# Value product copies, a weight rest and a rotary sum placed elsewhere in a two-layer encoder trunk

## The chip, the cores and the metric

The kernel runs on one core of a Trainium2 chip. The metric is the device time of one execution in microseconds (us), as the median of several runs. The engines are named as in the profile: PE is TensorE's matmuls and PEld its weight loads, DVE is VectorE, ACT is ScalarE, POOL is GpSimd and SP is SyncE, which here issues most of the transfers. PSUM is the memory that matmuls write to, and SBUF holds everything else on the core.

## The reference

Two layers over 512 tokens of width 1024, in fp32. Layer 0 mixes the tokens by neighbourhood attention with 16 heads of width 64, layer 1 by latent attention (MLA) with 16 heads, whose queries and shared key have a rotary part of width 32. In both, the mixer's output is multiplied by a gate `silu(z)` and projected. After each mixer comes a second gate that adds a projection of the per-layer input `p`.

```python
def apply_rope(x, cos, sin):
    x1, x2 = jnp.split(x, 2, axis=-1)
    ...
    return jnp.concatenate([x1 * c - x2 * s, x1 * s + x2 * c], axis=-1)

def mixer_na(xn, w_in, rpb, w_out):
    q, k, v, z = jnp.split(xn @ w_in, 4, axis=-1)
    o = neighbourhood_attention(q.reshape(shp), k.reshape(shp), v.reshape(shp), rpb)
    return (o.reshape(B, S, hd) * jax.nn.silu(z)) @ w_out

def reference(x, p, ...):
    for i in range(DEPTH):
        xn = rmsnorm(x, norm_g[i])
        y = mixer_na(...) if i % 2 == 0 else mixer_mla(...)
        h = x + y
        gate = jax.nn.sigmoid(rmsnorm(h, ple_norm[i]) @ ple_w_gate[i])
        x = h + gate * (p[i] @ ple_w_proj[i])
    return rmsnorm(x, final_norm)
```

## The kernel before, in words

**Splits.** Every fp32 product is made of three matmuls in a faster type. A matrix is split into a rounded copy (`hi`) and what is left (`lo`), and hi·hi, lo·hi and hi·lo are summed in a PSUM bank. ACT usually makes the copy. What is left, called the rest here, is one subtraction on DVE or POOL. For weights `load_w` does this: a transfer on SP's queue into a raw tile (`wraw`, three buffers), a copy on ACT (L100), a rest on POOL or, where `rest` says so, on DVE (L101).

**PSUM.** `psum(tag)` hands out the banks: two for `mm`, two for `S`, three for `T`, one for `O`. A new tile in a tag waits until the tile that had its bank has been read.

**Who sets the order.** The program is written as a Python function whose statements are in a chosen order. A scheduler with a time model then sets the order of each engine's queue from the dependencies, the priorities that follow from the order of the statements, and explicit `issue_after` ties. Within a queue an engine goes strictly in order, so an instruction that waits holds everything behind it.

**Layer 0's values.** The value projection is computed as seven products of half the size (`values_seven`, L261 to L410), after the scheme of Strassen: weights and inputs are first mixed (sums and differences), the products are numbered 1 to 7, and the four quarters of the result are put together from them by adding and subtracting whole PSUM banks. `made(p, c, ...)` splits piece c (0 or 1) of product p's weight into copy (ACT) and rest (DVE, two instructions). `product(p)` issues 24 matmuls, the first 12 into the bank of half 0 and the others into that of half 1 (L301). Products 5 and 3 add onto the banks of product 6, product 4 onto those of product 7. So before product 5 may add onto a bank of product 6, that bank's content has to be kept: `after6` copies it to SBUF on ACT (`s6`) and subtracts it from product 7's bank on DVE. `after7` adds `s1` to product 7's bank on DVE and copies the sum out on ACT (`s17`). Nearly all of these copies and rests stand on L51, the line of a helper; they are told apart by their tiles. `pair.rests(1)` makes the rests of a pair of heads' queries and keys.

**Layer 0's heads.** Sixteen heads in pairs (`na_head`, L536 to L609); heads are numbered from 0 here. A head works in two halves. PE makes scores into an `S` bank (L558, L559), DVE adds the bias and finds the maxima (L565, L568), ACT exponentiates and sums (L576), DVE takes the reciprocal of two sums at a time (L578), POOL multiplies by it (L582, two instructions for each half). PE then transposes the result into `T` banks (L594, L596), ACT and DVE split them (`ph`, `pl`, L110 and L112), and PE multiplies by the values into the `O` bank (L608). From there ACT copies (L220), DVE adds (L221), and POOL multiplies by the gate and splits (L225, L229, `oh` and `ol`). PE's queue is filled between these steps with matmuls of other work. `out_proj` (L622 to L637) loads four weight pieces for each of two column halves n, pieces c = 1 and 3 with their rests on DVE, and makes eight products (`ps_mm`, `ps_S`, `ps_T`, `ps_O`) out of `oh` and `ol`.

**Layer 1's rotary part.** For each of four groups of heads, `rope(g)` (L980 to L999) turns a PSUM tile of queries: a copy (L992, ACT), an exchange of neighbours (L993, DVE), two multiplications by the tables of cosines and sines (L994 on DVE; L995 on DVE for g = 0, else POOL), their sum (L996, POOL), the split into a copy (L997, ACT) and a rest (L998, POOL). SP then moves the parts of `rh` and `rl` to the tiles of the single heads (`qe`, `qo`, L117). The scores of the first heads of layer 1 (PE, L123, `ps_S<-ke,qe`) use them.

Of the kernel before, what the change touches and what calls it, by code (L numbers as in the profile page):

```python
# [16 lines left out]
ALU = mybir.AluOpType  # L17
# [39 lines left out]
class Trunk:  # L57
# [28 lines left out]
        return t  # L86


    def load_w(self, ap, n, extra=False, parts=1, rest=None, late=None):

        nc = self.nc
        pool = self.wx if extra else self.wp
        raw = self.wp.tile([P, 1024], F32, name="wraw", tag="wraw", bufs=3)
        tags = ("w4", "w4") if extra and self.wxn > 5 else ("whi", "wlo")
        hi, lo = (pool.tile([P, n if extra else 1024], F32R, name="whi"[:1] + t, tag=t, bufs=self.wxn if extra else 3)
                  for t in tags)
        w = n // parts
        for c in [slice(i * w, (i + 1) * w) for i in range(parts)]:
            self.last_load = nc.sync.dma_start(raw[:, c], ap[:, c])
            nc.scalar.activation(hi[:, c], raw[:, c], AF.Copy)  # L100
            f = lambda e, c=c: e.tensor_tensor(out=lo[:, c], in0=raw[:, c], in1=hi[:, c].bitcast(F32), op=ALU.subtract)  # L101
            if late is not None and c.stop == n:
                late.append(lambda: f(nc.gpsimd))
            else:
                f(rest or nc.gpsimd)
        return hi, lo


# [158 lines left out]
    def values_seven(self, pool, xT, xk, Q, pair, more):  # L267

        nc = self.nc
# [49 lines left out]
        def after7(i):  # L319
            self.dve.tensor_tensor(out=C[7, i], in0=C[7, i], in1=s1[i], op=ALU.add)  # L320
            s17[i] = copy("s17", i, C[7, i])

        def after6(i):
            s6[i] = copy("s6", i, C[6, i])
            sub(C[7, i], C[7, i], s6[i])

        def after5(i):
# [53 lines left out]
        product(7)  # L381
        pair.keys(1)
        made(5, 1, T[5][:, 1, :])
        after7(0)
        after7(1)
        made(4, 0, T[7][:, 0, :], True)
        pair.rests(1)
        product(6)
        after6(0)
        after6(1)  # L390
        made(4, 1, T[7][:, 1, :], True)
        made(3, 0, self.raw_piece(1, 2))
        product(5)
# [142 lines left out]
    def na_head(self, pool, h, sq, s0, dk, kl, vh):  # L536
# [9 lines left out]
        for half in range(2):  # L546
            sp = self.psum("S")
            for i in range(2):
                qt = 2 * half + i
                o = sp[:, i * 256:(i + 1) * 256]  # L550
                if qt == 0:
                    o = o.rearrange("p (a b) -> p a b", a=2)
                    lq = s0
                    K = lambda t: win(t, 0, P, 0, [[384, 2], [1, P]])
                else:
                    lq = sq[:, qt * P - 64:qt * P + 64]
                    K = lambda t: t[:, (qt - 1) * P:(qt + 1) * P]
                nc.tensor.matmul(o, lq, K(dk), start=True, stop=False)  # L558
                nc.tensor.matmul(o, lq, K(kl), start=False, stop=True)  # L559
            for i in range(2):  # L560
                qt = 2 * half + i
                c = slice(qt, qt + 1)
                if qt == 0:
                    for r, sc in ((slice(0, 64), slice(0, 128)), (slice(64, 128), slice(128, 256))):
                        nc.vector.tensor_tensor_reduce(out=ex[r, 0:P], in0=sp[r, sc], in1=bias[r, 0:P], scale=-1.0,  # L565
                                                       scalar=-NEG, op0=ALU.add, op1=ALU.min, accum_out=mx[r, c])
                else:
                    nc.vector.tensor_tensor_reduce(out=ex[:, ecol(qt)], in0=sp[:, i * 256:(i + 1) * 256],  # L568
                                                   in1=bias[:, P:], scale=-1.0, scalar=-NEG, op0=ALU.add, op1=ALU.min,
                                                   accum_out=mx[:, c])  # L570
            hs = slice(2 * half, 2 * half + 2)
            for i in range(2):
                qt = 2 * half + i
                e = ex[:, ecol(qt)]
                with self.tc.issue_after(self.hold):
                    self.last_exp = nc.scalar.activation(e, e, AF.Exp, scale=-1.0, bias=mx[:, qt:qt + 1],  # L576
                                                         accum_out=sm[:, qt:qt + 1])
            nc.vector.reciprocal(rc[:, hs], sm[:, hs])  # L578
            for i in range(2):
                qt = 2 * half + i  # L580
                e = ex[:, ecol(qt)]
                self.last_norm = nc.gpsimd.tensor_tensor(out=e, in0=e, in1=rc[:, qt:qt + 1].to_broadcast([P, e.shape[1]]),  # L582
                                                         op=ALU.mult)
# [21 lines left out]
        n = 0  # L605
# [16 lines left out]
    def out_proj(self, wap, oT, res, after, last_mm):  # L622
        nc = self.nc
        for n in range(2):
            ws = [self.load_w(wap[n, c], 1024, extra=n == 1 or c == 3, rest=nc.vector if self.wxn > 5 and c % 2 else None)
                  for c in range(4)]
            for u, t in enumerate(range(NT)):
                ps = self.psum(("mm", "mm", "S", "S", "T", "O", "mm", "mm")[n * NT + u])
# [313 lines left out]
    def mla_heads(self, pool, xT, cT, sets, oT):  # L942
# [42 lines left out]
        def rope(g, a0, a1):  # L985
# [7 lines left out]
            nc.vector.stream_shuffle(sw, xr, swap)  # L993
            nc.vector.tensor_tensor(out=xr, in0=psr, in1=rc_t, op=ALU.mult)  # L994
            (nc.gpsimd if g else nc.vector).tensor_tensor(out=sw, in0=sw, in1=rs_t, op=ALU.mult)  # L995
            nc.gpsimd.tensor_tensor(out=sw, in0=xr, in1=sw, op=ALU.add)  # L996
            nc.scalar.activation(rh, sw, AF.Copy)  # L997
            A["rl", g] = nc.gpsimd.tensor_tensor(out=rl, in0=sw, in1=rh.bitcast(F32), op=ALU.subtract)  # L998
            R[g] = rh, rl  # L999
# [475 lines left out]
```

## Time and profile before

| | us |
|---|---|
| median of 3 runs | 653.1 (652.88 to 653.74) |
| profiled execution | 653.56 |
| its span (first to last instruction) | 651.5 |
| PE busy | 640.2 |
| DVE busy | 427.7 |
| ACT busy | 453.4 |
| POOL busy | 408.4 |

The granted TensorE clock was 0.995 of full speed. The view of waits gives, for each group of instructions, the time that its engine sat idle, who released it, how often, and the longest. A row of the timeline has the start in us from the span's start, the time from start to end of the group, the engine, the line and the operation with its output and inputs, how many instructions are joined in the row, and in brackets the idle time before it with its releaser. Matmuls overlap, so that their starts are closer together than their durations. SPq is SP's queue of transfers: a row there is the issue.

### The profile page before, as it was taken

To read this page: it belongs to the slowest core of one execution; us is meant where nothing else is said; L and a number is where in the kernel's file an instruction comes from. 1 tells how busy PE (TensorE), PEld (TensorE's weight loads), DVE (VectorE), ACT (ScalarE), POOL (GpSimd) and SP (SyncE) were. 2 spreads that over 40 slices of the span, in tenths; PEclk is the share of its full clock that TensorE was granted. 3 is DMA by queue.
4 is the path that set the end of the run, shared out by engine and by line. 5 is a ranking of instruction groups with operands and counts; after the bars stand their busy time and mean duration, and the time that the engine had idled before them with its cause. 6 is when DMAs were issued, how large, how long until landed. Compare 5 with 4: busy or idle time off the path is not lost.

```text
span 651.5 us, 9980 instructions
## 1 busy us (share of the span) xinstructions
PE 640.2 (98%) x3299; PEld 541.9 (83%) x3299; DVE 427.7 (66%) x886; ACT 453.4 (70%) x903; POOL 408.4 (63%) x371
## 2 busy tenths in 40 slices
PE   9999999999999999999999999999999999999994
PEld 6888878888888888888999887888888888888884
DVE  6197987565665616569715514898988885474665
ACT  7575766887886733788644535897989897547855
POOL 0471006877978853797655516786969887437974
PEclk9999999999999999999999999999999999999997
DMA  9939725778958989446643245120112223683524
GB/s 326 355 124 306 217 66 179 263 205 217 229 209 217 239 178 342 147 154 188 224 140 102 78 109 156 32 75 24 49 50 66 65 84 112 229 292 126 193 65 162
DMA packets 46131, 107.41 MB, mean 165 GB/s; under 512 B 4736, under 2 KB 17792, under 8 KB 46080
## 3 DMA queue, kind: packets, MB, share of 16 engines
q1 hardware_dynamic: 34608, 87.12, 39.3%
q0 software_dynamic: 11040, 18.88, 13.6%
q10 hardware_dynamic: 432, 0.79, 0.3%
q8 instruction: 26, 0.43, 0.3%
q14 instruction: 25, 0.20, 0.1%
HBM read 95.23 MB, written 25.17 MB: 185 GB/s over the span
## 4 chain that ended last, share of the span: by engine, by line
PE 83%; POOL 1%; ACT 1%; DVE 0%; DMA 0%; issue 0%; POOLq 0%
PE ps_mm L123 27%; PE ps_S L123 10%; PE ps_mm L959 7%; PE ps_T L155 6%; PE ps_T L851 5%; PE ps_O L1071 5%; PE ps_mm L851 3%; PE ps_S L851 3%; PE ps_O L608 2%; PE ps_T L123 2%; PE ps_O L123 2%; PE ps_mm L909 2%; PE ps_T L301 2%; PE ps_T L596 2%; PE ps_S L909 1%; PE ps_S L559 1%
## 5 line engine op out<-in xcount | busy, mean ns | idle before, releaser
L101 POOL TENSOR_TENSOR wwlo<-wraw,wwhi 128x1024 fp32r<-128x1024 f32 (+5 forms) x68 | 122.3, 1810 | 93.5 <-ACT wwhi L100 41.9
L796 POOL TENSOR_TENSOR wlo<-wraw,whi 128x512 fp32r<-128x512 f32 x56 | 72.7, 1331 | 22.3 <-ACT whi L794 20.2
L1056 POOL TENSOR_TENSOR ex<-ex,rc 128x512 f32<-128x512 f32 x64 | 66.2, 1043 | 26.6 <-DVE rc L1055 22.5
L100 ACT ACTIVATE wwhi<-wraw 128x1024 fp32r<-128x1024 f32 (+5 forms) x71 | 55.1, 799 | 34.3 <-PE ps_mm L123 18.9
L1054 ACT ACTIVATE ex<-ps_S,mx 128x512 f32<-128x512 f32 x64 | 44.0, 687 | 12.6 <-DVE mx L1052 10.9
L1052 DVE TENSOR_REDUCE mx<-ps_S 128x1 f32<-128x512 f32 x64 | 43.7, 683 | 8.4 <-PE ps_S L123 7.7
L582 POOL TENSOR_TENSOR ex<-ex,rc 128x128 f32<-128x128 f32 (+1 forms) x64 | 37.5, 701 | 17.7 <-DVE rc L578 17.5
L112 DVE TENSOR_TENSOR pt_lo<-ps_T,pt_hi 128x512 fp32r<-128x512 f32 x64 | 43.1, 680 | 7.1 <-ACT pt_hi L110 6.7
L110 ACT ACTIVATE pt_hi<-ps_T 128x512 fp32r<-128x512 f32 x64 | 37.7, 594 | 3.4 <-PE ps_T L155 3.0
L155 PE MATMUL ps_T<-ident,ex 128*128 128x128 f32 x256 | 38.3, 272 | 0.0
L155 PEld LDWEIGHTS ps_T<-ident,ex 128*128 128x128 f32 x256 | 31.5, 140 | 7.5
L123 PE MATMUL ps_mm<-xh,wwhi 128*128 128x512 f32 x120 | 33.7, 404 | 0.0
L221 DVE TENSOR_TENSOR u<-ps_O,u 64x512 f32<-64x512 f32 x32 | 21.9, 685 | 17.7 <-ACT u L220 17.2
L576 ACT ACTIVATE ex<-ex,mx 128x128 f32<-128x128 f32 (+1 forms) x64 | 30.2, 473 | 4.2 <-DVE mx L565 4.1
L123 PE MATMUL ps_mm<-xl,wwhi 128*128 128x512 f32 x120 | 31.9, 395 | 0.0
L794 ACT ACTIVATE whi<-wraw 128x1024 fp32r<-128x1024 f32 x28 | 29.3, 1057 | 3.2 <-DMA wraw<-sum 2.4
L123 PE MATMUL ps_mm<-xh,wwlo 128*128 128x512 f32 x120 | 31.1, 394 | 0.0
L123 PE MATMUL ps_S<-ke,qe 96*128 96x512 f32 x96 | 28.9, 407 | 0.3 <-DMA qe<-rl 0.3
L123 PE MATMUL ps_S<-ko,qo 128*128 128x512 f32 x96 | 28.9, 409 | 0.0
L959 PE MATMUL ps_mm<-cT,wwhi 128*128 128x512 f32 x94 | 27.7, 393 | 0.0
L220 ACT ACTIVATE u<-ps_O 64x512 f32<-64x512 f32 x32 | 18.9, 591 | 12.0 <-PE ps_O L608 8.8
L225 POOL TENSOR_TENSOR u<-u,z 128x512 f32<-128x512 f32 x16 | 22.6, 1412 | 7.5 <-DVE u L221 7.5
(488 smaller groups left out, 1915.1 us busy)
## 6 DMA issues: line engine op xcount, KB each, us to landing
sum<-gate POOLq DMA_DIRECT2D x12, 1024.0 KB, 8.2
wraw<-na_qk SPq DMA_DIRECT2D x16, 512.0 KB, 4.9
wraw<-sum SPq DMA_DIRECT2D x16, 512.0 KB, 3.3
pe<-pe SPq DMA_DIRECT2D x31, 256.0 KB, 5.9
wraw<-gate SPq DMA_DIRECT2D x12, 512.0 KB, 3.3
wraw<-na_v SPq DMA_DIRECT2D x10, 512.0 KB, 3.4
sum<-sum POOLq DMA_DIRECT2D x4, 1024.0 KB, 11.1
wraw<-na_o SPq DMA_DIRECT2D x8, 512.0 KB, 4.8
```

The source lines that it names most:

```text
L100: nc.scalar.activation(hi[:, c], raw[:, c], AF.Copy)
L101: f = lambda e, c=c: e.tensor_tensor(out=lo[:, c], in0=raw[:, c], in1=hi[:, c].bitcast(F32), op=ALU.subtract)
L110: self.last_copy = self.act.activation(hi, src, AF.Copy, scale=scale)
L112: self.dve.tensor_tensor(out=lo, in0=src, in1=hi.bitcast(F32), op=ALU.subtract)
L123: last = self.last_mm = nc.tensor.matmul(out, l, r, start=i == 0, stop=i == n - 1)
L155: self.last_mm = self.nc.tensor.transpose(t[:, i * P:(i + 1) * P], b, self.ident)
L796: nc.gpsimd.tensor_tensor(out=lo[:, o], in0=raw[:, o], in1=hi[:, o].bitcast(F32), op=ALU.subtract)
L851: mm = nc.tensor.matmul(ps, l, r, start=j == 0 and p in banks, stop=j == 11 and p in (2, 3, 4), skip_group_check=True)
L959: self.last_mm = nc.tensor.matmul(PS[key], *terms[i], start=i == 0, stop=i == len(terms) - 1)
L1052: nc.vector.reduce_max(mx, sp, axis=AX.X, negate=True)
L1054: nc.scalar.activation(ex, sp, AF.Exp, bias=mx, accum_out=sm)
L1056: nc.gpsimd.tensor_tensor(out=ex, in0=ex, in1=rc.to_broadcast([P, S]), op=ALU.mult)
```

## The change

It has three edits.

1. In `values_seven` product 6 is issued ahead of product 7's adds and copies, and its two copies are split off as `copy6(i)`. The first copy now comes ahead of both `after7`, the second behind them; the subtractions of `after6` follow, and piece 0 of product 4's weight comes last.
2. `load_w` gets an argument `behind`. In `out_proj` the rest of piece (n, c) = (0, 1) is tied behind `last_rc`, the last reciprocal that a head of layer 0 has issued. (In layer 1 that reciprocal is long past.)
3. In the first rope (g = 0) the sum of the two products is taken by DVE, not by POOL.

```diff
-    def load_w(self, ap, n, extra=False, parts=1, rest=None, late=None):
+    def load_w(self, ap, n, extra=False, parts=1, rest=None, late=None, behind=None):
...
-                f(rest or nc.gpsimd)
+                with self.tc.issue_after(behind) if behind is not None else nullcontext():
+                    f(rest or nc.gpsimd)
...
+        def copy6(i):
+            s6[i] = copy("s6", i, C[6, i])
+
         def after6(i):
-            s6[i] = copy("s6", i, C[6, i])
             sub(C[7, i], C[7, i], s6[i])
...
         made(5, 1, T[5][:, 1, :])
+        product(6)
+        copy6(0)
         after7(0)
         after7(1)
+        copy6(1)
+        after6(0)
+        pair.rests(1)
+        after6(1)
         made(4, 0, T[7][:, 0, :], True)
-        pair.rests(1)
-        product(6)
-        after6(0)
-        after6(1)
         made(4, 1, T[7][:, 1, :], True)
...
-            nc.vector.reciprocal(rc[:, hs], sm[:, hs])
+            self.last_rc = nc.vector.reciprocal(rc[:, hs], sm[:, hs])
...
             ws = [self.load_w(wap[n, c], 1024, extra=n == 1 or c == 3, rest=nc.vector if self.wxn > 5 and c % 2 else None,
+                              behind=self.last_rc.ins if (n, c) == (0, 1) and self.wxn > 5 else None)
                   for c in range(4)]
...
-            nc.gpsimd.tensor_tensor(out=sw, in0=xr, in1=sw, op=ALU.add)
+            (nc.gpsimd if g else nc.vector).tensor_tensor(out=sw, in0=xr, in1=sw, op=ALU.add)
```

The lines of the changed kernel stand one to six further down than those of the kernel before (L101 stays, L221 is L222, L578 is L583, L996 is L1002).

**ACT at product 6.** This is the difference of ACT's two queues at the end of the value products. `s_846` and `s_849` before, and `s_874` and `s_877` now, are the s17 copies of product 7's two halves; `s_884` and `s_887` before, and `s_871` and `s_879` now, are the s6 copies of product 6's two halves. `whi<-W_519` is the copy of a weight piece of product 4.

```order
 L51 ACTIVATE whi<-W_539 128x1024 [waits PE_49]
-L51 ACTIVATE s_846<-ps_T 128x512 [waits DVE_49]
-L51 ACTIVATE s_849<-ps_T 128x512 [waits DVE_49]
-L51 ACTIVATE whi<-W_519 128x1024
-L51 ACTIVATE s_884<-ps_T 128x512 [waits PE_49]
-L51 ACTIVATE s_887<-ps_O 128x512 [waits PE_49]
-L51 ACTIVATE whi<-W_519 128x1024
+L51 ACTIVATE s_871<-ps_T 128x512 [waits PE_49]
+L51 ACTIVATE s_874<-ps_T 128x512 [waits DVE_49]
+L51 ACTIVATE s_877<-ps_T 128x512 [waits DVE_49]
+L51 ACTIVATE s_879<-ps_O 128x512 [waits PE_49]
+L51 ACTIVATE whi<-W_519 128x1024 x2
```

The first s6 copy has moved from behind the s17 copies and a weight copy to the place ahead of them; the second now follows the s17 copies, and both weight copies come last.

**DVE at the last heads.** In the kernel before, DVE's queue from head 14's first reciprocal on; L101 is the rest of the output projection's piece (0, 1).

```order
L578 RECIPROCAL rc<-sm 128x2 [waits Activation_49]
L101 TENSOR_TENSOR wwlo<-wraw,wwhi 128x1024 [waits DMAHW2_49,PE_49]
L578 RECIPROCAL rc<-sm 128x2 [waits Activation_49]
L221 TENSOR_TENSOR u<-ps_O,u 64x512 [waits Activation_49]
L112 TENSOR_TENSOR pl<-ps_T,ph 128x2x192 [waits DVE_49,Activation_49]
```

In the changed kernel the same queue has head 14's two reciprocals together, and then these rows up to the maxima of head 15's first half (L570 and L573):

```order
L583 RECIPROCAL rc<-sm 128x2 [waits Activation_49] x2
L113 TENSOR_TENSOR pl<-ps_T,ph 128x2x192 [waits DVE_49,Activation_49]
L222 TENSOR_TENSOR u<-ps_O,u 64x512 [waits Activation_49]
L570 ISA ex,mx<-ps_S,bias 64x128 [waits DVE_49,DMAHW4_49,PE_49,Pool_49]
L570 ISA mx 64x1
L570 ISA ex,mx<-ps_S,bias 64x128
L570 ISA mx 64x1
L573 ISA ex,mx<-ps_S,bias 128x256
L573 ISA mx 128x1
```

Further on, behind both reciprocals of head 15, stands the rest, and behind that the output adds of heads 13 and 14:

```order
L113 TENSOR_TENSOR pl<-ps_T,ph 128x2x192 [waits DVE_49,Activation_49]
L113 TENSOR_TENSOR pl<-ps_T,ph 128x512 [waits Activation_49]
L583 RECIPROCAL rc<-sm 128x2 [waits Activation_49] x2
L101 TENSOR_TENSOR wwlo<-wraw,wwhi 128x1024 [waits DMAHW2_49]
L222 TENSOR_TENSOR u<-ps_O,u 64x512 [waits Activation_49] x2
```

The rest has left the place between head 14's two reciprocals and moved past the whole of head 15's first steps. From product 6 to the middle of layer 0's second gate, the rows of all engines are also interleaved a little differently; behind that their order is as before, but for the third edit.

**ACT at the first rope.** In the kernel before, ACT's queue from the copy of the rotary tile (L992) on; `ke` and `ko` are keys, `qe` and `qo` queries of a pair of heads.

```order
L992 ACTIVATE rh<-ps_mm 128x512 [waits PE_49]
L110 ACTIVATE ke_3473<-ps_S 64x512 [waits PE_49]
L110 ACTIVATE qe_3469<-ps_S 64x512 [waits PE_49]
L110 ACTIVATE ko_3475<-ps_S 64x512 [waits DVE_49]
L997 ACTIVATE rh<-rl 128x512 [waits Pool_49]
L110 ACTIVATE qo_3471<-ps_S 64x512 [waits DVE_49]
```

And in the changed kernel:

```order
L998 ACTIVATE rh<-ps_mm 128x512 [waits PE_49]
L111 ACTIVATE ke_3473<-ps_S 64x512 [waits PE_49]
L111 ACTIVATE qe_3469<-ps_S 64x512 [waits PE_49]
L1003 ACTIVATE rh<-rl 128x512 [waits DVE_49]
L111 ACTIVATE ko_3475<-ps_S 64x512 [waits DVE_49]
L111 ACTIVATE qo_3471<-ps_S 64x512 [waits DVE_49]
```

The copy of the rotary sum now waits for DVE instead of POOL, and stands one place further ahead. DVE has the sum (L1002) right behind L1001, the former L995.

More of the change, by code (lines that the diff above doesn't have):

```diff
@@ L624, in out_proj @@
         for n in range(2):
-            ws = [self.load_w(wap[n, c], 1024, extra=n == 1 or c == 3, rest=nc.vector if self.wxn > 5 and c % 2 else None)
+            ws = [self.load_w(wap[n, c], 1024, extra=n == 1 or c == 3, rest=nc.vector if self.wxn > 5 and c % 2 else None,
+                              behind=self.last_rc.ins if (n, c) == (0, 1) and self.wxn > 5 else None)
                   for c in range(4)]
```

## The prediction

> **What bounds the kernel now.** I read the page first, then the table of TensorE's waits, then the timeline around each place that the table names.
>
> ```profile
> span 651.5 us, 9980 instructions
> PE 640.2 (98%) x3299; PEld 541.9 (83%) x3299; DVE 427.7 (66%) x886; ACT 453.4 (70%) x903; POOL 408.4 (63%) x371
> ```
>
> TensorE (PE) is busy for 640.2 of 651.5 us; VectorE (DVE), ScalarE (ACT) and GpSimd (POOL) have 30 to 37% of the span free. The number and the shapes of its matmuls are the same before and after, so the change can only move time through PE's waits. These are all that the view of waits has:
>
> ```profile
> PE ps_T L301 <- ACT s L51: 1.2, 1, 1.2
> PE ps_T L1187 <- PEq L1464: 0.8, 1, 0.8
> PE ps_T L596 <- POOL ex L582: 0.3, 1, 0.3
> PE ps_S L123 <- DMA qe<-rl: 0.3, 1, 0.3
> ```
>
> The second is the start of the program. The other three are one wait each, and each of the three edits lies at one of them. So the most that the edits can win together is near 2 us of 653, about 0.3%; a measurement of this kernel tells about 0.2%, 1.3 us, from no change. The view counts a wait from the modelled end of the matmul before; what PE really loses is the distance between two starts beyond the usual one, and I take that below.
>
> **First edit: the order of the value products.** The timeline of before at the end of product 6:
>
> ```profile
> 83.94 1.07 PE L301 MATMUL ps_T<-whi,V 128*128 128x512 f32 x4
> 84.50 2.49 DVE L51 TENSOR_TENSOR wlo<-W,whi 128x512 fp32r<-128x512 f32 x4
> 84.84 0.62 PE L301 MATMUL ps_T<-wlo,V 128*128 128x512 f32 x2
> ...
> 86.91 1.29 DVE L51 TENSOR_TENSOR ps_T<-ps_T,s 128x512 f32<-128x512 f32 x2
> ...
> 87.63 1.20 ACT L51 ACTIVATE s<-ps_T 128x512 f32<-128x512 f32 x2 [2.49 <-DVE ps_T L51]
> 87.56 0.62 PE L301 MATMUL ps_O<-wlo,V 128*128 128x512 f32 x2
> ...
> 88.72 1.05 ACT L51 ACTIVATE whi<-W 128x1024 fp32r<-128x1024 f32 x1
> 88.73 0.28 PE L558 MATMUL ps_S<-da,sa 128*128 128x256 f32 x1
> ...
> 88.85 0.28 PE L559 MATMUL ps_S<-la,sa 128*128 128x256 f32 x1
> 89.67 0.59 ACT L51 ACTIVATE s<-ps_T 128x512 f32<-128x512 f32 x1
> ...
> 90.31 0.98 PE L301 MATMUL ps_T<-whi,V 128*128 128x512 f32 x3 [1.18 <-ACT s L51]
> ```
>
> Product 5 is the last row. It adds to the bank of product 6's first half, and may start once ACT has copied that bank out (s6, the row at 89.67). The half was complete at 84.84 + 0.62 = 85.46, but ACT sat idle for 2.49 us with the two s17 copies of product 7 at the head of its queue, waiting for DVE, and after them came the weight copy of 1.05. Score matmuls start every 88.85 − 88.73 = 0.12 us, so the next start was due at 88.97; it came at 90.31. Lost: 1.34 us.
>
> After the change s6(0) stands ahead of the s17 copies: it runs in the idle stretch, from about 85.5 to 86.1, and the s17 copies start at 87.63 as before. Product 5 then finds its bank free 2.9 us early. Next to become late would be its second half, which needs s6(1). That copy now comes straight behind the s17 copies: 88.83 + 0.59 = 89.42, while PE reaches that half after 12 matmuls of (84.84 − 83.94)/4 = 0.225 us, at 88.97 + 2.7 = 91.7. After that product 4's weights are due at 88.97 + 24 × 0.225 = 94.4. The weight copy moves behind s6(1), to 89.4–90.5. DVE has s6(1)'s subtraction ahead of the rest of that weight (to 90.1), then four rests of 2.49/4 = 0.62 each from 90.5: all done by 93.0. Both covers hold, by 2.3 and 1.4 us. No DMA is moved here: the weights of product 4 are already in SBUF. Gain 1.34; bounds 0 (another wait in the same place) and 1.34.
>
> **Second edit: the weight rest behind the last head's reciprocal.** The timeline around heads 14 and 15:
>
> ```profile
> 218.30 3.10 POOL L582 TENSOR_TENSOR ex<-ex,rc 128x128 f32<-128x128 f32 x4 [1.75 <-DVE rc L578]
> ...
> 218.43 1.35 DVE L101 TENSOR_TENSOR wwlo<-wraw,wwhi 128x1024 fp32r<-128x1024 f32 x1 [0.27 <-PE ps_mm L123]
> ...
> 218.68 0.18 ACT L576 ACTIVATION_READ_ACCUMULATOR ex<-ex,mx 128x1 f32 x1
> ...
> 218.81 0.28 PE L608 MATMUL ps_O<-ph,Q 128*128 128x256 f32 x1
> ...
> 218.92 0.28 PE L608 MATMUL ps_O<-pl,Q 128*128 128x256 f32 x1
> ...
> 219.24 0.59 ACT L220 ACTIVATE u<-ps_O 64x512 f32<-64x512 f32 x1 [0.38 <-PE ps_O L608]
> ...
> 219.70 0.15 DVE L578 RECIPROCAL rc<-sm 128x2 f32<-128x2 f32 x1
> ...
> 219.87 0.68 DVE L221 TENSOR_TENSOR u<-ps_O,u 64x512 f32<-64x512 f32 x1
> ...
> 220.79 0.33 PE L608 MATMUL ps_O<-ph,Q 128*128 128x192 f32 x1
> ...
> 220.94 0.27 DVE L565 CUSTOM_DVE_ANT_0 ex<-ps_S,bias 64x128 f32<-64x128 f32 x1
> ...
> 221.45 0.33 PE L596 MATMUL ps_T<-ident,ex 128*128 128x128 f32 x1 [0.33 <-POOL ex L582]
> ...
> 221.57 0.42 DVE L568 CUSTOM_DVE_ANT_0 ex<-ps_S,bias 128x256 f32<-128x256 f32 x1
> ```
>
> The sums for head 14's second reciprocal were ready at 218.86, but DVE was 1.35 us deep in the rest, so the reciprocal ran at 219.70, POOL multiplied late, and the transpose at 221.45 was due at 220.90 (small matmuls start every 0.11 us, as 218.81 to 218.92). Lost: 0.55. With the rest gone from there, the reciprocal can run 0.8 us earlier: this wait goes, gain 0.55.
>
> The edit also reorders the last heads, and something else comes near. In the new order the first output-projection product (into ps_S) waits for DVE's maxima of head 15's first half, and these stand behind a head's output add. From the last ps_O matmul of that head to the product, PE has ten transposes and five output matmuls at 0.11 and five score matmuls at 0.12: 2.25 us. DVE's way there is the rest of that matmul, 0.17, the copy 0.59, the add 0.68, the maxima 221.57 + 0.42 − 220.94 = 1.05, and three handovers of 0.04: 2.6. That is a new wait of about 0.35; the bounds are 0 (ACT and DVE get to it a little sooner) and 0.7 (another 0.35 of queue in ACT, half a copy). I take 0.35, because the rows add up to it. Net gain 0.2, between −0.15 and 0.55.
>
> The rest itself, 1.35 on DVE, now stands behind both reciprocals of head 15, and behind it the output adds of heads 13 and 14, which free the one ps_O bank. By the same counting DVE finishes the first of them 1.9 us before PE wants the bank; that cover would have to go first. Its raw tile comes free later by some 4 us, and SP's next load into such a tile waits for another rest anyway.
>
> **Third edit: the rotary sum.** The timeline of the first rope:
>
> ```profile
> 393.70 2.40 POOL L101 TENSOR_TENSOR wwlo<-wraw,wwhi 128x1024 fp32r<-128x1024 f32 x1 [1.16 <-ACT wwhi L100]
> ...
> 394.91 0.69 DVE L994 TENSOR_TENSOR rh<-ps_mm,rope_c 128x512 f32<-128x512 f32 x1
> ...
> 395.52 1.13 DVE L995 TENSOR_TENSOR rl<-rl,rope_s 128x512 f32<-128x512 f32 x1
> ...
> 396.57 0.68 DVE L112 TENSOR_TENSOR ke<-ps_S,ke 64x512 fp32r<-64x512 f32 x1
> 396.73 1.29 POOL L996 TENSOR_TENSOR rl<-rh,rl 128x512 f32<-128x512 f32 x1 [0.63 <-DVE rl L995]
> ...
> 398.05 0.63 ACT L997 ACTIVATE rh<-rl 128x512 fp32r<-128x512 f32 x1 [0.17 <-POOL rl L996]
> ...
> 398.76 1.29 POOL L998 TENSOR_TENSOR rl<-rl,rh 128x512 fp32r<-128x512 f32 x1 [0.74 <-ACT rh L997]
> ...
> 400.08 0.51 SPq L117 DMA_DIRECT2D qe<-rl  x1
> ...
> 401.14 0.63 PE L123 MATMUL ps_S<-ke,qe 96*128 96x512 f32 x2
> ...
> 402.07 0.50 PE L123 MATMUL ps_S<-ke,qe 96*128 96x512 f32 x1 [0.30 <-DMA qe<-rl]
> ```
>
> The third score matmul was due at 401.14 + 2 × 0.23 = 401.60 and started at 402.07, when the transfer of rl had landed: lost 0.47. The chain ran L995, L996, L997, L998, transfer. The sum of 1.29 us on POOL, ended at 398.02, becomes one on DVE. Its price lies between 0.69 (L994, one operand in PSUM) and 1.13 (L995, both in SBUF, beside POOL's L101). I take 0.69: at 396.65 POOL's L101 is over (396.10), and what POOL does next waits for this sum. So it ends at 397.34, the copy and the transfer come 0.68 earlier, and rl lands near 401.39: the wait goes, gain 0.47. At 1.13 they come 0.24 earlier and 0.24 is won. DVE's ke and qe rests slide 0.69 and still end before 399, ahead of 401.14; ACT takes the rope copy first and ko behind it.
>
> [...]
>
> **Sum.** 1.34 + 0.2 + 0.47 = 2.0 us. The profiled execution took 653.56 (span 651.5), 0.46 above the median of 653.1, so I set the gain against the median: 651.1. It passes to the end, since after each place PE has no other wait, and a transfer released by an engine moves forward with it.
>
> **Rivals.**
> - *All three waits go and no new one comes.* For it: the 0.35 at the projection is a difference of two sums of 2.25 and 2.6. 2.36 won: 650.7. Chance 0.2.
> - *Much of it is given back.* Either product 5 is held as before (s6(0) not early, because ACT is busy there: 653.1 − 0.7 = 652.4), or the heads, whose rows between product 6 and the gate are interleaved anew, open waits like the 0.55 at two or three of 32 halves (652.2 to 652.7). Against it: ACT's 2.49 idle, and one wait in 32 before. Chance 0.25, within 0.2%.
> - *Slower: a weight rest between a head's multiplies.* In the new order POOL does such a rest between the two pairs of multiplies of a head in five heads, before in two; the rests take 2.40 (row at 393.70). If the second pair is needed at once, PE's transposes wait for the whole rest. One in full leaves 651.1 + 2.4 = 653.5, no change; two decide: 655.9. Against it: the two heads that had this before show no wait. Chance 0.08.
>
> My forecast has the other 0.47. Range: 650.4 (the first rival less a measurement's 0.3) to 652.5 (most of the second). Faster 0.67, same 0.25, slower 0.08.
>
> **What would show it.** Product 5 should follow the scores with no gap, s6(0) being done before 86.5. No transpose near 221 should wait for POOL; a wait of 0.2 to 0.5 of the first ps_S product for DVE is my new term. The first rope's score matmuls should run without a gap, the sum on DVE at about 0.69. I am wrong if product 5 still waits, or if transposes in the middle heads wait for POOL.

## The result and the profile after

| | before | after |
|---|---|---|
| median, runs taken together (us) | 653.11 (652.58 to 655.17, 10 runs) | 651.31 (651.21 to 651.58, 10 runs) |
| ratio after to before, 95% interval | | 0.9971 [0.9961, 0.998] |
| profiled execution (us) | 653.56 | 651.45 |
| its span (us) | 651.5 | 649.3 |
| granted TensorE clock | 0.995 | 0.996 |

The changed kernel is 1.8 us faster in the median. A run's time is 1.8 to 2.4 us longer than its span, and the kernels differ in this: 2.1 in all runs of after, 2.0 in the median of before's. No instruction of the kernel lies there, so for differences of a few tenths the text goes by the traces and spans. The page of after begins so:

```profile
span 649.3 us, 9981 instructions
PE 639.7 (99%) x3299; PEld 541.9 (83%) x3299; DVE 429.6 (66%) x887; ACT 454.6 (70%) x903; POOL 407.3 (63%) x370
```

PE has the same 3299 matmuls, in a span that is 2.2 us shorter. The view of PE's waits has one row, the start of the program; the three waits of before have gone.

```profile
PE ps_T L1193 <- PEq L1470: 0.8, 1, 0.8
```

That view counts idle time only, and leaves small waits out. For the sum I took the distance between two matmul starts, less the usual distance of that shape, and added it up by stretches of the span. This is my own sum over the starts in the two traces, in us; the last column is what the prediction gave.

| stretch (us of the span) | before | after | won | predicted |
|---|---|---|---|---|
| 0 to 10, start | 0.48 | 0.34 | 0.14 | - |
| 80 to 92, place 1 | 1.47 | 0.00 | 1.47 | 1.34 |
| 110 to 235, heads and place 2 | 1.25 | 1.44 | -0.19 | 0.2 |
| 390 to 404, place 3 | 0.58 | -0.01 | 0.59 | 0.47 |
| all others | 2.76 | 2.66 | 0.10 | - |

So places 1 and 3 paid, and the heads paid nothing. A wait also has a tail: the matmul behind the one that waited starts some 0.34 us after it, where 0.227 is usual (at product 5 in before, 0.341). That is why the table has 1.47 and 0.58 for before where the prediction counted 1.34 and 0.47 at the waiting matmul alone.

**Place 1.** The timeline of after, from the end of product 6's first half (first row) to product 4 (last row):

```profile
84.70 0.62 PE L302 MATMUL ps_T<-wlo,V 128*128 128x512 f32 x2
...
85.35 0.60 ACT L51 ACTIVATE s<-ps_T 128x512 f32<-128x512 f32 x1 [0.84 <-PE ps_T L302]
...
87.00 1.20 ACT L51 ACTIVATE s<-ps_T 128x512 f32<-128x512 f32 x2 [1.05 <-DVE ps_T L51]
...
88.09 0.59 ACT L51 ACTIVATE s<-ps_O 128x512 f32<-128x512 f32 x1
...
88.70 0.28 PE L564 MATMUL ps_S<-la,sa 128*128 128x256 f32 x1
...
88.82 1.09 PE L302 MATMUL ps_T<-whi,V 128*128 128x512 f32 x4
...
90.39 2.50 DVE L51 TENSOR_TENSOR wlo<-W,whi 128x512 fp32r<-128x512 f32 x4
...
91.57 1.07 PE L302 MATMUL ps_O<-whi,V 128*128 128x512 f32 x4
...
94.29 0.62 PE L302 MATMUL ps_T<-whi,xh 128*128 128x512 f32 x2
```

s6(0) runs at 85.35 in ACT's idle stretch. Product 5 starts at 88.82, 0.12 behind the last score matmul: no gap. Both covers held: s6(1) is done at 88.68, 2.9 us ahead of the half that needs it (91.57); product 4's rests are done at 92.89, 1.4 ahead of product 4.

**Place 2.** The timeline of after around head 14's two reciprocals (first row), head 15's (the last but two) and the first output projection product (L124, `ps_S`):

```profile
214.74 0.46 DVE L583 RECIPROCAL rc<-sm 128x2 f32<-128x2 f32 x2
...
215.04 2.12 POOL L587 TENSOR_TENSOR ex<-ex,rc 128x128 f32<-128x128 f32 x4 [0.77 <-DVE rc L583]
...
218.58 0.56 DVE L113 TENSOR_TENSOR pl<-ps_T,ph 128x384 fp32r<-128x384 f32 x1 [3.38 <-ACT ph L111]
...
220.44 0.42 DVE L573 CUSTOM_DVE_ANT_0 ex<-ps_S,bias 128x256 f32<-128x256 f32 x1
...
220.47 0.31 PE L613 MATMUL ps_O<-ph,Q 128*128 128x256 f32 x1
...
220.92 0.73 PE L124 MATMUL ps_S<-wwhi,oh 128*128 128x512 f32 x2
...
223.14 0.21 DVE L583 RECIPROCAL rc<-sm 128x2 f32<-128x2 f32 x2
...
223.27 1.20 DVE L101 TENSOR_TENSOR wwlo<-wraw,wwhi 128x1024 fp32r<-128x1024 f32 x1
...
223.44 3.01 POOL L587 TENSOR_TENSOR ex<-ex,rc 128x128 f32<-128x128 f32 x4 [3.87 <-DVE rc L583]
```

POOL now multiplies for head 14 right behind both reciprocals, and no transpose waits for it. The new wait is there: the product at 220.92 was due at 220.47 + 0.11 = 220.58 and waited for the maxima at 220.44, which is 0.34 (and 0.11 more at the start behind it). The rest stands behind head 15's reciprocals, beside POOL's four multiplies, which take 3.01 there against 2.12 without a neighbour. DVE's 3.38 us of idle time ahead of 218.58 matters below.

**Place 3.** The timeline of after at the first rope:

```profile
390.29 1.06 ACT L100 ACTIVATE wwhi<-wraw 128x1024 fp32r<-128x1024 f32 x1 [0.81 <-PE ps_mm L965]
...
393.25 1.12 DVE L1001 TENSOR_TENSOR rl<-rl,rope_s 128x512 f32<-128x512 f32 x1
...
394.41 0.69 DVE L1002 TENSOR_TENSOR rl<-rh,rl 128x512 f32<-128x512 f32 x1
...
397.17 0.51 SPq L118 DMA_DIRECT2D qe<-rl  x1
...
399.56 0.86 PE L124 MATMUL ps_S<-ke,qe 96*128 96x512 f32 x3
```

The three score matmuls follow each other without a gap, and the sum on DVE takes 0.69, as assumed. But the issue of `qe<-rl` stands 399.56 − 397.17 = 2.39 us ahead of the first score, against 401.14 − 400.08 = 1.06 in before. That is 1.33 earlier, and the sum explains 1.29 − 0.69 = 0.6 of it. Something else has moved as well, and the experiments had to find it.

### The profile page after: what moved, and what is told of

It reads as the page before. It is cut to its first block, busy times and chain, and to the rows that moved or that the text cites. A ratio compares the mean times of both kernels' runs of the same rounds, so it can differ in the third digit from the quotient of the medians.

```text
span 649.3 us, 9981 instructions
## 1 busy us (share of the span) xinstructions
PE 639.7 (99%) x3299; PEld 541.9 (83%) x3299; DVE 429.6 (66%) x887; ACT 454.6 (70%) x903; POOL 407.3 (63%) x370
## 4 chain that ended last, share of the span: by engine, by line
PE 98%; ACT 1%; DVE 0%; issue 0%; POOLq 0%; POOL 0%; DVEq 0%; ACTq 0%
PE ps_mm L124 28%; PE ps_S L124 12%; PE ps_mm L965 7%; PE ps_T L156 6%; PE ps_T L857 5%; PE ps_O L1077 5%; PE ps_mm L857 3%; PE ps_mm L418 3%; PE ps_T L302 3%; PE ps_S L857 3%; PE ps_T L124 3%; PE ps_O L124 2%; PE ps_O L613 2%; PE ps_mm L915 2%; PE ps_S L302 2%; PE ps_mm L201 2%
## 5 line engine op out<-in xcount | busy, mean ns | idle before, releaser
L101 POOL TENSOR_TENSOR wwlo<-wraw,wwhi 128x1024 fp32r<-128x1024 f32 (+5 forms) x68 | 121.1, 1795 | 96.5 <-ACT wwhi L100 45.6
L100 ACT ACTIVATE wwhi<-wraw 128x1024 fp32r<-128x1024 f32 (+5 forms) x71 | 55.1, 799 | 33.9 <-PE ps_mm L124 18.0
L124 PE MATMUL ps_mm<-xh,wwhi 128*128 128x512 f32 x120 | 33.2, 401 | 0.0
L222 DVE TENSOR_TENSOR u<-ps_O,u 64x512 f32<-64x512 f32 x32 | 22.0, 686 | 16.7 <-ACT u L221 15.8
L124 PE MATMUL ps_mm<-xl,wwhi 128*128 128x512 f32 x120 | 32.5, 399 | 0.0
L124 PE MATMUL ps_mm<-xh,wwlo 128*128 128x512 f32 x120 | 31.1, 394 | 0.0
L124 PE MATMUL ps_S<-ko,qo 128*128 128x512 f32 x96 | 28.9, 409 | 0.0
L124 PE MATMUL ps_S<-ke,qe 96*128 96x512 f32 x96 | 28.6, 406 | 0.0
L124 PEld LDWEIGHTS ps_mm<-xh,wwlo 128*128 128x128 f32 x120 | 22.0, 188 | 4.6
```

Source lines behind the costliest of these rows:

```text
L124: last = self.last_mm = nc.tensor.matmul(out, l, r, start=i == 0, stop=i == n - 1)
```

## The experiments

Twelve kernels were run. Each row has the kernel before as it was timed beside it.

| run | median (us), runs | before (us) | ratio, 95% |
|---|---|---|---|
| e1_values: edit 1 alone | 652.05, 11 | 653.05 | 0.9987 [0.9978, 0.9996] |
| e2_rest: edit 2 alone | 652.36, 11 | 653.05 | 0.9989 [0.998, 0.9998] |
| e12_no_rope: edits 1 and 2 | 651.38, 9 | 653.05 | 0.9975 [0.9966, 0.9985] |
| e13_no_rest: edits 1 and 3 | 651.53, 11 | 653.05 | 0.9977 [0.9969, 0.9986] |
| e3_rope: edit 3 alone | 653.21, 11 | 652.94 | 1.0002 [0.9993, 1.0011] |
| e12_warm14 | 651.56, 10 | 652.94 | 0.9975 [0.9965, 0.9986] |
| s6_late | 652.43, 1 | 652.94 | - |
| copy_only | 651.66, 1 | 652.94 | - |
| before_late | 655.16, 5 | 652.90 | 1.0031 [1.0017, 1.0046] |
| after_late | 651.19, 10 | 652.90 | 0.9975 [0.9965, 0.9984] |
| before_warm8 | 658.77, 4 | 652.94 | 1.0087 [1.0064, 1.011] |
| e12_warm12 | 651.55, 10 | 652.94 | 0.9981 [0.9972, 0.999] |

The same sum over matmul starts, for the stretches that matter, in us lost:

| run | start | 80 to 92 | 150 to 217 | 217 to 235 | 300 to 350 | 390 to 404 |
|---|---|---|---|---|---|---|
| before | 0.48 | 1.47 | 0.28 | 0.67 | 0.39 | 0.58 |
| after | 0.34 | 0.00 | 0.47 | 0.66 | 0.36 | -0.01 |
| e1_values | 0.53 | 0.00 | 0.48 | 0.67 | 0.67 | -0.02 |
| e2_rest | 0.38 | 1.00 | 0.29 | 0.35 | 0.35 | 0.35 |
| e3_rope | 0.25 | 1.64 | 0.28 | 0.63 | 0.38 | -0.02 |
| e12_no_rope | 0.54 | 0.00 | 0.45 | 0.64 | 0.35 | 0.00 |
| e13_no_rest | 0.33 | 0.00 | 0.47 | 0.67 | 0.74 | -0.02 |

### Each edit alone

e1_values, e2_rest and e3_rope have one edit of the diff each, and leave the other two out.

> Edit 1 alone. Theory A, each edit removes its own wait: product 5 starts without a gap (1.34 us won), the waits near 221 us (0.55) and at the first rope (0.47) stay: 653.1 - 1.3 = 651.8. Theory B, edit 1 carries most of it: in the order that the scheduler makes of edit 1 the rest already stands behind both of head 14's reciprocals, in a stretch where DVE of the changed kernel is idle for 3.4 us, so the wait near 221 is gone as well; and the rope chain of the changed kernel began 0.7 us earlier against PE, before its sum, because a weight had come in sooner; if that belongs to edit 1 too, the rope waits no more and the time is 651.0 to 651.3.

> Edit 2 alone. Theory A: the wait of 0.55 near 221 us goes and the one of 0.34 at the projection comes: 0.2 won, 652.9. A rival: the new wait at the projection belongs to the order that edit 1 makes, and here 0.55 is won: 652.55. The waits at product 5 (1.34) and at the rope (0.47) stay in both.

> Edit 3 alone; PE's order is that of before. The load of the weight that ACT copies ahead of the rotary tile should again be held at its issue for 1.7 to 2.0 us (387.3 in before), so the chain starts as late as in before, and only the shorter sum can help: the transfer is issued 0.65 to 0.7 earlier against PE and the wait of 0.47 at the rope goes. Theory A and theory B both say 653.05 - 0.47 = 652.6; a rival, that the sum on DVE is as dear as L995 (1.13), leaves 0.2 of the wait: 652.8.

Edit 1 alone wins place 1 and also place 3, whose code it does not touch. Edit 2 alone wins 0.3 at place 2. In its trace, the loss at place 1 is smaller than before's, which it doesn't touch either. In edit 3's trace the wait at place 3 is gone, but the time shows no gain. Two things are in that: its time is 2.4 us longer than its span, where before has 2.0, and its trace loses 0.17 more at place 1. (Nor does the trace show that edit 3 took the wait away: the table under place 3 has the reason.) So the three effects don't add up, and two questions follow: what else sets place 3, and why does place 1 differ between kernels with the same order there?

### Two edits together

e12_no_rope and e13_no_rest are the changed kernel with one edit taken back.

```diff
-            (nc.gpsimd if g else nc.vector).tensor_tensor(out=sw, in0=xr, in1=sw, op=ALU.add)
+            nc.gpsimd.tensor_tensor(out=sw, in0=xr, in1=sw, op=ALU.add)
```

> The change without edit 3 (the rotary sum stays on POOL). Theory A: the third score matmul of the first rope waits for the transfer of rl again, 0.47 us: 651.31 + 0.47 = 651.8. Theory B: the chain's earlier start (0.7) covers the sum's 1.29 on POOL instead of 0.69 on DVE, PE does not wait, and the time is that of the change, 651.3.

```diff
-            ws = [self.load_w(wap[n, c], 1024, extra=n == 1 or c == 3, rest=nc.vector if self.wxn > 5 and c % 2 else None,
-                              behind=self.last_rc.ins if (n, c) == (0, 1) and self.wxn > 5 else None)
+            ws = [self.load_w(wap[n, c], 1024, extra=n == 1 or c == 3, rest=nc.vector if self.wxn > 5 and c % 2 else None)
```

> The change without edit 2 (the rest is not tied). Theory A: the reciprocal is late again, a transpose waits for POOL for about 0.5 and the new wait of 0.34 at the projection goes: 651.4 to 651.5. Theory B: the rest falls into DVE's idle 3.4 us behind head 14's reciprocals and nobody waits for it; what is left is at most the 0.34 at the projection: 651.0 to 651.3.

Without edit 3 the time is 651.38, within what can be told of after's 651.31, and the scores of the first rope don't wait. So with edits 1 and 2 in place the sum on DVE is worth nothing that these runs can tell. The medians of e1_values and e13_no_rest, which also differ in edit 3 alone, are 0.5 apart; but the medians of their spans are 649.8 and 649.7, and the rest lies outside the span (2.27 and 1.80).

Without edit 2 no transpose waits for POOL either. The timeline of e13_no_rest shows why:

```profile
214.72 0.46 DVE L583 RECIPROCAL rc<-sm 128x2 f32<-128x2 f32 x2
...
215.02 2.12 POOL L587 TENSOR_TENSOR ex<-ex,rc 128x128 f32<-128x128 f32 x4 [0.77 <-DVE rc L583]
...
217.11 1.23 DVE L101 TENSOR_TENSOR wwlo<-wraw,wwhi 128x1024 fp32r<-128x1024 f32 x1 [1.92 <-PE ps_mm L124]
...
220.90 0.72 PE L124 MATMUL ps_S<-wwhi,oh 128*128 128x512 f32 x2 [0.15 <-DVE mx L573]
```

Edit 1's own order of the heads already puts both of head 14's reciprocals ahead of the rest, and the rest falls into DVE's idle time, the stretch that is 3.38 us long in after. The product at 220.90 waits as it does in after, so the new wait of 0.34 comes with edit 1's order and not with edit 2; e2_rest has no such wait. What e1_values and e13_no_rest have is another 0.3 to 0.4 lost between 316 and 321 us, in the second gate of layer 0. There DVE's rest of the inputs starts 0.7 us later (315.50 in e13_no_rest, 314.76 in after). I didn't trace where that delay begins.

### Place 1: what the copy's early place buys

s6_late puts the first s6 copy back behind the s17 copies; copy_only leaves it early, and gives the second copy and the weight copy their old order.

```diff
         product(6)
-        copy6(0)
         after7(0)
         after7(1)
+        copy6(0)
         copy6(1)
```

> The change, but with both s6 copies behind both s17 copies; the weight copy of product 4 stays last. Theory of the prediction, the s6 copy has to fill ACT's idle time ahead of the s17 copies: a good part of the wait stays, as s17 ends only near 88.2 and s6(0) then takes 0.6, to 88.8 to 89.4 against 88.8 that PE wants: 0 to 0.6 lost. Rival, it was the weight copy of 1.05 between s17 and s6 that held product 5, and the early place adds little: no more than 0.1 lost at product 5.

```diff
         after7(1)
-        copy6(1)
-        after6(0)
+        made(4, 0, T[7][:, 0, :], True)
         pair.rests(1)
+        after6(0)
+        copy6(1)
         after6(1)
-        made(4, 0, T[7][:, 0, :], True)
```

> The change, but the weight copy of product 4, piece 0, stands ahead of the second s6 copy again; only the first s6 copy is early. Theory: product 5 needs only s6(0) at its start, and its second half comes 2.7 us later, when s6(1) is done even behind the weight copy (88.2 + 1.05 + 0.6 = 89.9 against 91.5): no wait at product 5 or its second half, and product 4's weight is earlier, too. Rival, s6(1) becomes the bound: a wait of 0.3 or more at product 5's second half.

By the sum over the starts, s6_late lost 0.91 at product 5 and copy_only nothing. So the first copy's early place is enough by itself. The weight copy's place counts too: in s6_late it no longer stands ahead of s6(0), and product 5 starts 1.73 behind the start of the s17 copies (87.94 and 89.67), against 2.68 in before (87.63 and 90.31). Had the s17 copies started at 87.00, as in after, s6_late's product 5 could have started at 88.73 by this distance and would not have waited (an estimate). Its 0.91, more than the 0 to 0.6 expected, came with a load that was late. Where that lateness comes from is next.

The difference between e2_rest (0.89 lost at product 5) and e3_rope (1.52), which have the same order here, begins 22 us earlier. First e2_rest, then e3_rope: ACT's copy of a weight piece, the s17 copies, and product 5.

```profile
64.58 1.06 ACT L51 ACTIVATE whi<-wraw 128x1024 fp32r<-128x1024 f32 x1
...
87.08 1.20 ACT L51 ACTIVATE s<-ps_T 128x512 f32<-128x512 f32 x2 [2.48 <-DVE ps_T L51]
...
89.76 1.20 PE L302 MATMUL ps_T<-whi,V 128*128 128x512 f32 x4 [0.73 <-ACT s L51]
```

```profile
65.08 1.06 ACT L51 ACTIVATE whi<-wraw 128x1024 fp32r<-128x1024 f32 x1 [0.55 <-DMA wraw<-na_qk]
...
87.58 1.20 ACT L51 ACTIVATE s<-ps_T 128x512 f32<-128x512 f32 x2 [2.49 <-DVE ps_T L51]
...
90.26 0.96 PE L302 MATMUL ps_T<-whi,V 128*128 128x512 f32 x3 [1.36 <-ACT s L51]
```

In e3_rope the copy at 65.08 waited 0.55 for a transfer. It starts 0.50 later than in e2_rest; the s17 copies start 0.50 later, and so does product 5. (The two losses differ by another 0.14, because in e3_rope PE itself was due that much earlier.) From that copy on, ACT and DVE hand work to each other with no slack: in all twelve traces without added work the s17 copies start 22.48 to 22.52 behind it. So a late load arrives at product 5 in full, and the 1.34 of before is one draw out of these.

In e12_no_rope the load was as late, and nothing came of it:

```profile
65.42 1.06 ACT L51 ACTIVATE whi<-wraw 128x1024 fp32r<-128x1024 f32 x1 [0.61 <-DMA wraw<-na_qk]
...
85.54 0.60 ACT L51 ACTIVATE s<-ps_T 128x512 f32<-128x512 f32 x1
87.92 1.20 ACT L51 ACTIVATE s<-ps_T 128x512 f32<-128x512 f32 x2 [1.78 <-DVE ps_T L51]
```

s6(0) at 85.54 doesn't wait for the end of that chain. This also fits the scatter: the ten runs of before spread over 2.6 us, and those of after over 0.4.

The next pair tests it on purpose. In both kernels the chain is made longer by two DVE instructions, which repeat two weight rests with the same values.

```diff
         made(7, 0, T[7][:, 0, :], True)
+        for o in (slice(0, S), slice(S, 2 * S)):
+            self.rest(*W[7][0], T[7][:, 0, :], o)
```

> The kernel before, with the two rests of product 7's first weight piece made twice by VectorE (the same values again; 2 x 0.62 us more in DVE's queue, some 20 us ahead of product 5). Theory, DVE's and ACT's chain from about 66 us on has no slack until the s6 copy, so whatever comes late there comes out at product 5: its wait grows by about 1.2 from the 0.9 to 1.5 of the runs without it, to 2.1 to 2.7, and the time by as much, to 654.2. Rival, the chain has slack on the way (ACT waits for DVE near 76 us): the wait stays near 1.3 and the time at 653.0.

> The changed kernel with the same two rests made twice. Theory, the first s6 copy no longer stands behind that chain, and the second has 2.5 us to spare: product 5 starts without a wait, and the time is the changed kernel's within 0.3, 651.3 to 651.6 (product 4's weights, 1.4 to spare, are the next that could be late). Rival, the cover only moved: a wait of about 1 us comes at product 5's second half or at product 4, and the time is 652.3.

With after's order there was no wait, and the time is 651.19. With before's the time is 655.16; the execution that was profiled is the slowest of its five, 656.78. The timeline of before_late has the same three rows, and four later matmuls for comparison:

```profile
66.09 1.06 ACT L51 ACTIVATE whi<-wraw 128x1024 fp32r<-128x1024 f32 x1 [1.37 <-DMA wraw<-na_qk]
...
89.81 1.20 ACT L51 ACTIVATE s<-ps_T 128x512 f32<-128x512 f32 x2 [2.49 <-DVE ps_T L51]
...
92.49 2.08 PE L301 MATMUL ps_T<-whi,V 128*128 128x512 f32 x4 [3.36 <-ACT s L51]
...
96.91 1.08 PE L301 MATMUL ps_O<-whi,V 128*128 128x512 f32 x4
```

By the sum over the starts product 5 lost 3.52, 2.18 more than the 1.34 of before. The s17 copies (87.63 in before) come 89.81 − 87.63 = 2.18 later, to the hundredth the same. The two rests are 1.2 of it. The other 0.96 is the load, for which ACT waited 1.37 here: its copy starts at 66.09, in before at this row. (The row names PE, but the load landed at 65.03, and in the traces in which this copy waited it starts 0.1 behind the landing.)

```profile
65.13 1.06 ACT L51 ACTIVATE whi<-wraw 128x1024 fp32r<-128x1024 f32 x1 [0.37 <-PE ps_S L301]
```

The wait then cost a second time. The first four matmuls of product 5 took 2.08 us from the first start to the last end, against 1.08 for the four at 96.91. In before_late's table by stretch, the last three numbers are the granted clock, the share of DMA and its GB/s:

```profile
92.00:96.00 4.00, 3.51 (x9) 2.81 (x10) 3.92 (x7) 2.81 (x4) 0.00 (x0) 0.57 0.00 0
```

The clock was 0.57, and from 92 to 110 us 1.69 more was lost.

### Place 3: a fetch of PE's own program

The trace lists the transfers by queue, and one queue of after's page carries instructions:

```profile
q8 instruction: 26, 0.43, 0.3%
```

That is 26 packets of 16 KB for PE's 6598 matmuls and weight loads, one for each 254 of them (the expectations below say 256). The packets come all along the program at about this distance, so I take them for PE's instructions. In the fourteen traces 44 issues of SP take 1.2 to 2.0 us, and each of them begins within 0.3 us of such a packet and ends 0.15 to 0.4 us behind the packet's end; of the others nearly all take 0.3 to 0.7 (40 take up to 1.1, some of them far from any packet). First before, then after, at the loads ahead of the first rope:

```profile
387.29 1.98 SPq L99 DMA_DIRECT2D wraw<-mla_z  x1
```

```profile
385.71 0.53 SPq L99 DMA_DIRECT2D wraw<-mla_z  x1
386.28 1.42 SPq L954 DMA_DIRECT2D rope_c<-rope_c  x1
```

In before the packet holds the load of a weight whose copy on ACT (L100) stands ahead of the rotary tile's copy. That copy is this row of before:

```profile
392.56 1.06 ACT L100 ACTIVATE wwhi<-wraw 128x1024 fp32r<-128x1024 f32 x1 [1.50 <-POOL wwlo L101]
```

The view names POOL's L101, which ended at about the same moment. But the load landed at 392.46, and in all five traces in which L100 came late it starts 0.10 behind the landing; in after it starts 0.67 ahead of the end of that L101. L100 starts 8.58 us ahead of the first rope score in before, and in after (390.29) 9.27 ahead: 0.69 earlier. In after the packet comes 0.7 us later in the program and holds a table that nobody is waiting for yet. The reading is that edit 1, through the order of PE's instructions, moved a fetch off the load that mattered. With 11 warm-up matmuls the packet comes 61 matmuls ahead of the first rope score in all four traces without edit 1, and 58 ahead in all seven with it; which change in the order makes these three matmuls isn't shown. Three kernels tested the reading by the number of warm-up matmuls at the start of the program, which should shift PE's later fetches. Their result is read by nothing.

```diff
-NWARM = 11
+NWARM = 14
```

That is e12_warm14, made from e12_no_rope; e12_warm12 has 12 there, and before_warm8 is the kernel before with 8.

> The change without edit 3, and with 14 instead of 11 warm-up matmuls at the very start (three more that compute nothing; PE's stream is six instructions longer from there on). Fetch theory: the 16 KB packets of PE's instructions come once in 256 of its instructions, so the one near 386 us comes three matmuls, 0.7 us, earlier against PE, and the transfer that SP is issuing at that moment is held for 1.4 to 2.0 us: now the load of the weight (as in before), not the table of cosines behind it. Then the rope chain starts 0.5 to 0.7 later and the wait at the rope is back, 0.2 to 0.47: 651.6 to 651.9, if the start takes no longer. Rival, the chain's start has to do with edit 1's order and not with the fetch: no wait at the rope, 651.4.

> The kernel before with three fewer warm-up matmuls at the start of the program (8 instead of 11; their result is read by nothing). No line of the rotary part is touched. Theory (place 3 hangs on where PE's own program is fetched): a packet of the queue that carries PE's instructions comes once in some 256 PE instructions, so with three warm-ups fewer it comes 0.7 to 1.2 us later in the program. In the kernel before it held the issue of mla_z's weight load (1.98 us); now that issue takes 0.5 to 0.6 and the issue of rope_c or rope_s behind it is held 1.3 to 2.0 instead. ACT's copy of that weight and with it the rotary copy come 0.5 to 0.7 us earlier against PE, and the wait of 0.47 of the first rope's third score matmul is gone (0 to 0.1) with the sum still on GpSimd. Rival (the sum on GpSimd is the cause): the wait stays at 0.4 to 0.5. The first stretch of the program may change by up to 1 us either way, since the warm-ups stand there; place 1 scatters as in the other kernels without edit 1 (0.9 to 1.6).

> The changed kernel without edit 3, with one warm-up matmul more (12 instead of 11). Theory (fetch): against 11 warm-ups the packet of PE's instructions near 386.5 comes 0.25 to 0.45 us earlier, which is inside the 0.57 us in which SP issues mla_z's weight load; so that issue is held 1.4 to 2.0 us, ACT's copy of the weight comes later against PE than the 9.27 us ahead of the first rope's scores, at 8.6 to 9.0, and the wait of the third score matmul comes back, 0.1 to 0.47; with it the time 0.1 to 0.5 above the changed kernel without edit 3. Rival (edits 1 and 2 move ACT's or DVE's queue for some other reason, and the fetch has no part): mla_z's issue and the wait stay as with 11, 0.53 and 0.

e12_warm14: the held issue moved 1.2 us earlier, to a `qo` transfer ahead of the weight load (1.77 us), by more than I had reckoned. L100 came 0.22 later than in e12_no_rope, and the third score 0.01 late, with 0.11 more at the start behind it: the fetch moved as the theory says, but the load was just in time, so that this run decided little on the wait.

before_warm8 did decide it. Its timeline at the first rope, with the sum still on GpSimd:

```profile
392.71 0.53 SPq L99 DMA_DIRECT2D wraw<-mla_z  x1
...
393.78 1.59 SPq L949 DMA_DIRECT2D rope_s<-rope_s  x1
...
397.29 1.06 ACT L100 ACTIVATE wwhi<-wraw 128x1024 fp32r<-128x1024 f32 x1 [0.81 <-PE ps_mm L959]
...
401.47 1.29 POOL L996 TENSOR_TENSOR rl<-rh,rl 128x512 f32<-128x512 f32 x1 [0.63 <-DVE rl L995]
...
404.82 0.51 SPq L117 DMA_DIRECT2D qe<-rl  x1
...
406.56 0.86 PE L123 MATMUL ps_S<-ke,qe 96*128 96x512 f32 x3
```

The packet holds `rope_s` now, L100 stands 406.56 − 397.29 = 9.27 ahead, and the three scores run without a gap. The wait of 0.47 is gone with no line of the rotary part touched. (Its time is 5.8 us longer, for other reasons. 2.3 of them are in the first 10 us, where the first product waits 0.98 and the matmuls from 5.90 to 8.46 us start 0.43 apart instead of 0.227, at a granted clock of 1.00 between 5 and 9 us. 1.7 lie between 10 and 80 us. At place 1 product 5 waits 2.1, and the matmuls behind it are slow for another 1.7.)

e12_warm12 is half a miss. The hold fell on the weight load as forecast:

```profile
385.99 1.50 SPq L99 DMA_DIRECT2D wraw<-mla_z  x1
...
390.64 1.06 ACT L100 ACTIVATE wwhi<-wraw 128x1024 fp32r<-128x1024 f32 x1 [0.89 <-DMA wraw<-mla_z]
...
399.84 0.86 PE L124 MATMUL ps_S<-ke,qe 96*128 96x512 f32 x3
```

L100 now waits for that load, but it stands 9.20 us ahead, only 0.07 later than without the hold, and no wait returned. In five of the fourteen traces the packet fell on this load. It was held for different times, and the delay follows the hold:

| run | hold of the weight load (us) | L100 ahead of the first score | lost at the third score |
|---|---|---|---|
| e3_rope (sum on DVE) | 1.44 | 9.27 | 0 |
| e12_warm12 | 1.50 | 9.20 | 0 |
| e2_rest | 1.72 | 8.80 | 0.24 |
| before_late | 1.84 | 8.76 | 0.29 |
| before | 1.98 | 8.58 | 0.47 |

In eight of the other nine traces L100 stands 9.27 ahead, and they lost nothing there; in the ninth, e12_warm14, where the packet came just ahead of this load, 9.05, and it lost the 0.01. A hold of 1.5 makes the load just late, and one of 1.98 costs 0.47. In e3_rope the hold was too short to delay L100, so its vanished wait says nothing on the sum on DVE. Place 3 was lost to the packet on this load and the length of its hold together. A longer hold goes with a longer packet (1.66 us on its queue in before, 1.26 in e3_rope); why a packet takes longer at one time than at another stays open.

## Why the prediction was right, and where it was not

**First edit.** Right in its mechanism, its size (1.34 at product 5) and both covers. It took the 1.34 for a fixed cost; with the arrival of a load 22 us earlier it is 0.9 to 2.1 in the four traces with before's order and no added work. The early copy makes product 5 independent of that load (e12_no_rope, after_late).

**Second edit.** The 0.55 went, and the new wait at the output projection came at 0.34 against 0.35 forecast. The step that failed is the net gain of 0.2: from 110 to 235 us the changed kernel loses 0.19 more than before. Some 0.2 is spread over the middle heads (150 to 217 us: 0.28 before, 0.47 after), in differences of under 0.1 each, and the same in every kernel with edit 1; another 0.2 lies between 217 and 235, 0.11 of it at the start behind the new wait. The prediction's second rival named new waits in the heads as the danger, but at 0.5 a place; it was many small ones. What makes up the rest is left open. The prediction also credited edit 2 with the 0.55. Alone it does win 0.3, but with edit 1 in, the wait would have gone without it (e13_no_rest).

**Third edit.** The price on DVE (0.69) and the disappearance of the wait were right; the cause was wrong. "The chain ran L995, L996, L997, L998, transfer" began too late: ahead of L995 stood a weight copy that waited for a held load, and that hold is what went. That the wait of 0.47 went as forecast was luck in this sense. POOL's sum took 1.29 in before and just as long in before_warm8, e12_no_rope and e12_warm12; with the load in time, the issue of `qe<-rl` comes 1.75 us ahead of the scores on POOL (e12_no_rope, before_warm8) and 2.39 on DVE. Before's third score needed it 1.53 ahead: it was issued at 1.06 and the score came 0.47 late (e12_warm14, at 1.52, agrees: 0.01 late). So both suffice. On before's late load the sum on DVE would also have sufficed by these rows, 1.06 + 0.64 = 1.70, but no run had both a load that late and the sum on DVE.

In after the sum took 0.69 with POOL idle beside it, while L1001, with POOL's L101 (391.42 to 393.82) beside it for half of its time, took 1.12 again. What the sum takes beside a working POOL, these rows don't show.

**The sum.** 1.34 + 0.2 + 0.47 = 2.0 was forecast. Places 1 to 3 gave 1.47 − 0.19 + 0.59 = 1.87, and the start of the program and small differences the rest of the 2.2 between the two spans. The medians differ by 1.8.

## What to carry to other kernels

A copy that only frees a bank belongs ahead of copies that wait for another engine, and its worth is not only the wait in one profile: it cuts the bank loose from everything that can be late upstream. When a wait of half a microsecond vanishes in a place that an edit touches, undo that edit alone before crediting it, since a reordering far upstream can move a transfer or a fetch by as much. And follow a chain back until something on it has slack: the rotary chain's cause stood four instructions ahead of where I began.

## What the runs showed of the hardware

A packet of the instruction queue, by its spacing (one for each 254 matmuls and weight loads) the fetch of PE's own program, held SP's issue of an unrelated transfer: at the weight load of `mla_z` the issue took 0.53 us without a packet and 1.4 to 2.0 with one. Another number of warm-up matmuls moved the packet near the first rope: against the first score it came 0.9 us earlier with one more, 1.2 earlier with three more and 1.1 later with three fewer.

PE's granted clock was lower behind two of the waits at product 5. After 1.95 us of idle time in the timeline (before_warm8) and after 3.36 (before_late), about eight matmuls started 0.43 us apart instead of 0.227, at a granted clock of 0.74 and 0.57 between 92 and 96 us; after 1.36 (e3_rope) none did, at 1.00. The slow stretch behind the wait lasted 3.5 us by the starts in before_warm8 and in before_late.
